# A bounded look-ahead for three engines between the gate stage and the second merge, and another order of the output's loads and last rows

## The chip, the cores and the metric

One core of a Trainium2 chip runs the whole kernel in one launch. The engines of the core have a queue of instructions each: TensorE (PE: matmuls, with its weight loads shown as PEld), VectorE (DVE), ScalarE (ACT), GpSimd (POOL) and SyncE (SP, which here only issues DMAs). The metric is the device time of one execution in microseconds. Each engine executes its queue in the order in which the kernel's scheduler has put it there; what an instruction at the head of a queue waits for, everything behind it waits for too.

## The reference

One step of a hybrid flow-matching backbone with a single layer, for 128 context tokens ("prompt") and 2048 latent tokens ("sample"), model width 1024. One input projection feeds three mixers of width 512:

```python
xn = rmsnorm(x, ln_g) * (1 + scale) + shift
qkv, beta, dec, z_a, u_b, v_b, z_b, x_c, z_c, gates = split(xn @ w_in)
# A: gated DeltaNet in chunks, forwards and backwards over the tokens, 4 heads of 128
#    S_t = a_t (I - b_t k_t k_t^T) S_{t-1} + b_t k_t v_t^T,   o_t = S_t^T q_t
o_a = rmsnorm(o) * silu(z_a)
o_b = u_b * (w_spatial @ rmsnorm(v_b) + b_spatial) * silu(z_b)   # chunks of 128 tokens
o_c = fourier(x_c) * silu(z_c)                                   # real part of a 2D (+ channel) FFT
merged = sum_n sigmoid(gates_n) * (o_n @ w_branch_n)
y = rmsnorm(x + gate * (merged @ w_out), final_g)
```

Results are y for both groups and the last states of the context scan.

## The kernel before

All big products are done in pairs of float16 (a high and a low half, three matmuls for one): `xh`, `xl` hold the modulated tokens, `whi`, `wlo` one block of 128 columns of a weight, scaled by a power of two that is found from the block's sum of squares. A weight block thus goes through a DMA, a square on ACT, a sum by one small matmul (`wscb`, `ones`), a few VectorE steps and the two conversions before TensorE may use it.

The stages follow each other on TensorE:

1. Prelude and SiLU gate stage (`silu_za`, `finish`), up to line 786: ACT, VectorE and TensorE are *kept* in written order here, by the wrapper `_InTurn`.
2. Decays and convolutions, the spatial mixer (`silu_unit`, `gate_unit`), the Fourier mixer (its tiles are `xc`, `Y1`, `X2`, `us`, `yT`; `halves_of` splits into pairs), then `merge(1)` and `merge(2)`, which multiply branch blocks (`big`) with `bhi`, `blo`, apply sigmoid gates `sg` and add rows `mrow`.
3. Beside all this runs `delta()`, a generator whose parts `pace.tick` and `pace.part` strew between the matmuls of stage 2. It first makes the triangular matrices (`n`, `T`, `tok`, inverted by VectorE in steps over `XB` and `E`, and stored as `ES`), then scans: for each of 34 chunks `S,sk` (state times keys), `v,R` (solve), `u,kn` (new state) are dependent matmuls with VectorE and ACT steps between them (`sv`, `u`, `S`), and `u,sqk`, `S,sq` and `finish(t, o)` make the output: squares `oss` on ACT, a power on GpSimd, scaling `o` on ACT, transposes on TensorE.
4. `merge(0)` and the output stage: eight pairs of token tiles (`two_tiles`), each a product of `pa` (merged, in seven linear combinations) with `wohi`, `wolo` or sums `tw` of the weight's quarters, then gate, residual, norm and store. The prompt's rows come last (`prompt_right`).

Between line 787 and the end the order on each engine is decided by the framework's scheduler, which has a timeline model: an instruction is put into its queue when the model says that its operands are there, so that instructions written much later can get ahead of earlier ones. `tc.high_priority()` moves one up; `tc.issue_after(x)` keeps an instruction behind `x` in its queue. The wrapper uses that:

```python
        def call(*args, **kw):
            with self.tc.issue_after(self.last.ins) if self.last is not None else ExitStack():
                self.last = f(*args, **kw)
```

In the output stage the loads at its start are chained by `in_turn`, which orders each SP load behind the one before. In the issue order on SP a load also waits until the load eight places earlier has landed.

Of the kernel before, what the change touches and what calls it, by code (L numbers as in the profile page):

```python
# [14 lines left out]
AF = mybir.ActivationFunctionType  # L15
ALU = mybir.AluOpType
# [4 lines left out]
P = 128  # L21
# [167 lines left out]
def hybrid_flow_kernel(ctx: ExitStack, tc: tile.TileContext, x_prompt, x_sample, state_delta, c, c_ctx, w_ada,  # L189
                       b_ada, w_blk, w_bd, a_log, dt_bias, w_spatial, b_spatial, w_brb, w_outb, final_g, w_adb, cols, x_t, x_tp,  # L190
                       consts, consts16, y_prompt, y_sample, new_state, dbg=None):
    nc = tc.nc
    G, SY = nc.gpsimd, nc.sync
    V, A, PE = [_InTurn(tc, e_) for e_ in (nc.vector, nc.scalar, nc.tensor)]
    uid, rot = [0], [0]

    def nm(s):
# [1758 lines left out]
    def sums_of(q):  # L1956
        in_turn(tw[q].rearrange("p j l k c -> p j (l k c)"), tD[q])
# [35 lines left out]
    def two_tiles(t, pa, xr, hh, end):  # L1993


        pl = ps_d if odd_pair[0] else ps_mm
        odd_pair[0] ^= 1
        a, Y, X = [bank(pl, [P, 512]) for _ in range(3)]
        p1 = sb(ep, [P, 512], "sg", bufs=4)
        u2, u3 = [sb(ep, [P, 512], "st", bufs=3) for _ in range(2)]  # L2000

        def gated(j, cs):
            G.tensor_tensor(hh[j][:, cs], hh[j][:, cs], gb[:, cs], ALU.mult)
            G.tensor_tensor(hh[j][:, cs], hh[j][:, cs], xr[j][:, cs], ALU.add)
# [36 lines left out]
        with tc.high_priority():  # L2041
            gate_add(hh[1][:, left], Y, gb[:, left], p1)
            piece(1, 1, xr[1], hh[1], left, V)
        Z = bank(ps_mm, [P, 512])
        product(Z, pa, 6, quarter(4, 512), True)
        with tc.high_priority():
            made = gate_add(hh[0][:, right], Z, gb[:, right], u2)
            piece(0, 1, xr[0], hh[0], right, V)
        with tc.issue_after(made.ins):
            for j, i in ((1, 0), (0, 0), (1, 1), (0, 1)):  # L2050
                summed_up(j, i)
        for j in (1, 0):
            G.tensor_tensor(norms[:, j:j + 1], parts[j][:, 1:2], mhalf, ALU.pow)
            A.activation(hh[j], hh[j], AF.Copy, scale=norms[:, j:j + 1])
            SY.dma_start(y_sample[0, (t + j) * P:(t + j + 1) * P], hh[j])

    parts = [sb(op, [P, 3], f"part{j}", bufs=1) for j in range(3)]
    norms = sb(op, [P, 3], "norms", bufs=1)

    def piece(j, i, junk, h, cs, on):  # L2060
        squared = A.activation(junk[:, cs], h[:, cs], AF.Square, accum_out=parts[j][:, i:i + 1])
        if on is not None:
            on.tensor_tensor(h[:, cs], h[:, cs], fg[:, cs], ALU.mult)
        return squared

    def summed_up(j, i):
        q_ = parts[j]
# [2 lines left out]
        else:  # L2070
            V.tensor_scalar(q_[:, 0:1], q_[:, 0:1], 1.0 / D, EPS, ALU.mult, ALU.add)

    def gate_add(out, src, gate, other):
        V.tensor_tensor(out, src, gate, ALU.mult)
        return V.tensor_tensor(out, out, other, ALU.add)

    def prompt_left():
        ps = bank(ps_mm, [P, 512])
# [4 lines left out]
        A.activation(gp[0], x_left, AF.Square, accum_out=parts[2][:, 0:1])  # L2083

    def prompt_right():
        after = None
        for i, cs in ((1, slice(0, 384)), (2, slice(384, 512))):
            ps = bank(ps_mm, [P, cs.stop - cs.start])
            gemm_N(ps, *p16, wo, 512 + cs.start, cs.stop - cs.start)
            with tc.high_priority(), tc.issue_after(after.ins) if i > 1 else ExitStack():  # L2090
                after = gate_add(gp_right[:, cs], ps, gp_right[:, cs], x_right[:, cs])
                A.activation(x_right[:, cs], gp_right[:, cs], AF.Square, accum_out=parts[2][:, i:i + 1])
                (G if i == 1 else V).tensor_tensor(gp_right[:, cs], gp_right[:, cs], fg[:, 512 + cs.start:512 + cs.stop], ALU.mult)
# [7 lines left out]
        V.tensor_scalar(gp_right, gp_right, n_, None, ALU.mult)  # L2101
        SY.dma_start(y_prompt[0, :, right], gp_right)

    in_turn(x_left, xp_[0:P, left])
# [52 lines left out]
```

## Time and profile before

| | us |
|---|---|
| median of 3 runs | 2162.39 (2161.81 to 2163.25) |
| profiled execution | 2166.18 |
| its span in the trace | 2164.4 |
| PE busy | 2088.8 (97%) |
| DVE busy | 1357.1 (63%) |
| ACT busy | 1061.7 (49%) |
| POOL busy | 751.7 (35%) |

The profiled execution is 1.8 us longer than its span and 3.8 us longer than the median. TensorE is busy 97% of the span, so what can be saved at an unchanged number of matmuls lies in the 76 us in which it is idle and in the stretches in which the granted clock is below 1. By the page the mean granted clock is 0.991. In the trace's answers a wait is shown as "idle before <- releaser", where the releaser is the instruction or DMA that ended it.

### The profile page before, as it was taken

The numbers are of one execution on the slowest core, as the hardware profiler recorded it, in microseconds if no ns is written. First come the engines' busy times: TensorE is split into PE (matmuls) and PEld (weight loads), VectorE is DVE, ScalarE is ACT, GpSimd is POOL, SyncE is SP. The second block draws the span as 40 slices with busy tenths as digits, with TensorE's granted clock in tenths as the row PEclk, the third lists the DMA queues.
The fourth block names the chain that finished last, engine by engine and source line by source line (L and its number), as shares of the span: only waits on it lengthen the run. The fifth ranks groups of instructions, "written<-read, shape, count | busy, mean of one in ns | idle before, by whom it ended". The sixth has DMA issues, their size and how long they took to land.

```text
span 2164.4 us, 42587 instructions
## 1 busy us (share of the span) xinstructions
PE 2088.8 (97%) x16133; PEld 1197.1 (55%) x16133; DVE 1357.1 (63%) x3101; ACT 1061.7 (49%) x2457; POOL 751.7 (35%) x933
## 2 busy tenths in 40 slices
PE   7999999999999999999899999999999999999998
PEld 4455444455555677777455555566555444444444
DVE  6656754389878797466655546756555554666245
ACT  5554744476555664445544445656543343453112
POOL 0321332233333432443222233345443234334364
PEclk9999999999999999999899999999999999999999
DMA  9525732277776743444655555867664645456852
GB/s 350 218 77 195 258 114 89 82 230 218 247 228 218 236 147 93 125 146 120 224 175 168 162 172 166 269 211 213 191 189 135 204 167 177 166 196 241 329 204 103
DMA packets 222909, 403.24 MB, mean 186 GB/s; under 512 B 39720, under 2 KB 109632, under 8 KB 219888
## 3 DMA queue, kind: packets, MB, share of 16 engines
q1 hardware_dynamic: 167664, 290.84, 42.2%
q0 software_dynamic: 15216, 65.89, 8.0%
q10 hardware_dynamic: 39824, 43.79, 6.1%
q8 instruction: 127, 2.08, 0.4%
q14 instruction: 78, 0.64, 0.1%
HBM read 258.19 MB, written 142.24 MB: 185 GB/s over the span
## 4 chain that ended last, share of the span: by engine, by line
PE 47%; DMA 8%; DVE 5%; ACT 2%; issue 1%; POOL 1%; SPq 0%; POOLq 0%; DVEq 0%; ACTq 0%
PE b L244 47%; DMA st<-br 2%; DMA pa<-pa 1%; DMA ES<-ei 1%; DMA br<-o 1%; DMA xh<-in_x_sample_dram 1%; DMA ei<-XB 1%; DVE big L1684 1%; DMA mrg<-mrow 0%; DMA S<-in_state_delta_dram 0%; DMA skn<-kv 0%; ACT big L1683 0%; PE b L1373 0%; DMA sn<-n 0%; DVE sg L470 0%
## 5 line engine op out<-in xcount | busy, mean ns | idle before, releaser
L244 PE MATMUL b<-xh,whi 128*128 128x512 f16 (+1 forms) x1920 | 650.9, 348 | 4.7 <-DVE sg L1447 2.5
L244 PE MATMUL b<-xl,whi 128*128 128x512 f16 (+1 forms) x1920 | 651.2, 348 | 0.0
L244 PE MATMUL b<-xh,wlo 128*128 128x512 f16 (+1 forms) x1920 | 650.6, 348 | 0.0
L244 PEld LDWEIGHTS <-whi 128*128 128x128 f16 x3888 | 355.6, 98 | 328.4 <-issue 11.8
L244 PEld LDWEIGHTS <-wlo 128*128 128x128 f16 x1944 | 190.5, 98 | 175.4 <-issue 3.8
L244 PE MATMUL b<-big,bhi 128*128 128x512 f16 (+1 forms) x960 | 251.5, 348 | 3.9 <-ACT big L1683 3.2
L244 PE MATMUL b<-big,blo 128*128 128x512 f16 (+1 forms) x480 | 163.3, 347 | 0.0
L1727 POOL TENSOR_TENSOR mrow<-mrow,sg 128x512 f32<-128x512 f32 (+1 forms) x80 | 93.0, 1163 | 145.9 <-DVE sg L1726 105.2
L244 PEld LDWEIGHTS <-xh 128*128 128x128 f16 x1496 | 119.0, 99 | 31.7 <-issue 2.5
L244 PEld LDWEIGHTS <-bhi 128*128 128x128 f16 x960 | 86.9, 98 | 77.9 <-ACT big L1683 2.9
L947 POOL TENSOR_TENSOR cy<-cy,raw 128x545 f32<-128x545 f32 (+1 forms) x48 | 64.1, 1361 | 182.4 <-ACT raw L946 182.4
L244 PEld LDWEIGHTS <-xl 128*128 128x128 f16 x1068 | 99.0, 99 | 44.6 <-DMA tw<-tw 2.0
L1717 ACT ACTIVATE sg<-b,winv 128x512 f32<-128x512 f32 (+1 forms) x120 | 74.0, 617 | 95.4 <-PE b L244 94.8
L1181 POOL COPY T<-ES 32x256 f16<-32x256 f16 x68 | 30.6, 450 | 198.0 <-DMA ES<-ei 189.8
L244 PE MATMUL b<-whi,xh 128*128 128x128 f16 x544 | 95.4, 222 | 2.7 <-DVE yT L1633 2.0
L244 PE MATMUL b<-wlo,xh 128*128 128x128 f16 x544 | 95.4, 222 | 0.0
L244 PE MATMUL b<-whi,xl 128*128 128x128 f16 x544 | 95.4, 222 | 0.0
L322 DVE SCALAR_TENSOR_TENSOR wlo<-wst,wsc,whi 128x1024 f16<-128x1024 f32 x52 | 67.7, 1303 | 34.1 <-ACT whi L321 34.0
L321 ACT ACTIVATE whi<-wst,wsc 128x1024 f16<-128x1024 f32 x52 | 59.4, 1145 | 51.4 <-DVE wsc L272 49.5
L1726 DVE SCALAR_TENSOR_TENSOR sg<-b,binv,sg 128x512 f32<-128x512 f32 (+1 forms) x80 | 53.4, 669 | 36.4 <-PE b L244 33.2
L1288 POOL TENSOR_TENSOR skn<-skn,ed 128x512 f32<-128x512 f32 x34 | 38.0, 1116 | 109.6 <-DMA skn<-kv 104.5
L244 PEld LDWEIGHTS <-pa 128*128 128x128 f16 x420 | 41.4, 99 | 54.5 <-DMA pa<-pa 3.8
(526 smaller groups left out, 4313.6 us busy)
## 6 DMA issues: line engine op xcount, KB each, us to landing
wst<-in_w_blk_dram SPq DMA_DIRECT2D x58, 512.0 KB, 3.9
pa<-pa POOLq DMA_DIRECT2D x16, 896.0 KB, 4.6
qkv<-cy POOLq DMA_DIRECT2D x12, 1089.0 KB, 5.3
st<-br SPq DMA_DIRECT2D x48, 256.0 KB, 3.6
mrow<-mrg SPq DMA_DIRECT2D x16, 576.0 KB, 4.6
pa<-pa SPq DMA_DIRECT2D x5, 1792.0 KB, 8.6
dc<-dec SPq DMA_DIRECT2D x17, 512.0 KB, 4.7
kq<-qkv SPq DMA_DIRECT2D x34, 256.0 KB, 4.9
```

The costliest lines, as they stand in the source:

```text
L244: newest[0] = PE.matmul(out, l, r, start=start, stop=stop, skip_group_check=reopened)
L321: w.made = A.activation(w.hi, st, AF.Copy, scale=s)
L322: w.low = V.scalar_tensor_tensor(w.lo, st, s, w.hi, ALU.mult, ALU.subtract)
L947: G.tensor_tensor(y[:, c0:c1], y[:, c0:c1], raw[:, 1 + c0:1 + c1], ALU.mult)
L1181: G.tensor_copy(T16[rows(a0, b), :, :, b], ES[0:32, :, 2 * a0 + b, :, wT])
L1288: G.tensor_tensor(h3(kn_), h3(kn_), bc(ed[:, d, t, :], P), ALU.mult)
L1684: V.scalar_tensor_tensor(o16[:, 1, g, t0:t0 + tn], st, s, o16[:, 0, g, t0:t0 + tn], ALU.mult, ALU.subtract)
L1717: gated_[0] = A.activation(sg, ps, AF.Sigmoid, scale=gw.inv)
L1726: V.scalar_tensor_tensor(sg, ps, binv[:, 1:2], sg, ALU.mult, ALU.mult)
L1727: G.tensor_tensor(mr, mr, sg, ALU.add)
```

## The change

Four edits. **The windows.** `_InTurn` keeps a list of what it issued. With `kept` each instruction is ordered behind the last one as before; with a `window` of n it is ordered behind the n-th last. From the end of the gate stage to the end of `merge(2)` ACT and GpSimd have a window of 4 and VectorE of 6; GpSimd is wrapped for that. TensorE is left to the scheduler, as is the rest of the kernel. **The loads.** The second pair's `pa` load comes ahead of `fg`, and the loads of `gp_right` and `x_right` go behind the third pair. **The last pair.** ACT, VectorE and TensorE are kept in written order from the last pair's second half on; one gate product and sum goes to GpSimd, the multiplies by `fg` change engines and places, and each row's root stands right behind its sum. **The prompt's right half** is written in the same way: the three sums and the root come ahead of the last multiply.

```diff
 class _InTurn:
     def __init__(self, tc, engine):
-        self.tc, self.engine, self.kept, self.last = tc, engine, False, None
+        self.tc, self.engine, self.kept, self.window, self.newest = tc, engine, False, 0, []
+
+    @property
+    def last(self):
+        return self.newest[-1] if self.newest else None
     def __getattr__(self, name):
         f = getattr(self.engine, name)
-        if not self.kept:
+        back = 1 if self.kept else self.window
+        if not back:
             return f
         def call(*args, **kw):
-            with self.tc.issue_after(self.last.ins) if self.last is not None else ExitStack():
-                self.last = f(*args, **kw)
-            return self.last
+            with self.tc.issue_after(self.newest[-back].ins) if len(self.newest) >= back else ExitStack():
+                self.newest.append(f(*args, **kw))
+            return self.newest[-1]
...
-    G, SY = nc.gpsimd, nc.sync
-    V, A, PE = [_InTurn(tc, e_) for e_ in (nc.vector, nc.scalar, nc.tensor)]
+    SY = nc.sync
+    G, V, A, PE = [_InTurn(tc, e_) for e_ in (nc.gpsimd, nc.vector, nc.scalar, nc.tensor)]
...
     V.kept = A.kept = PE.kept = False
+    A.window = G.window = 4
+    V.window = 6
...
     inv_ = merge(2, False, inv_, finish_delta, then=(0, 17), step=norm_step)
     cs_.close()
+    A.window = G.window = V.window = 0
...
+        in_order(True)
         total(u2, X, u2)
-        gate_add(p1, p1, gb[:, left], xr[1][:, left])
-        gate_add(hh[1][:, right], hh[1][:, right], gb[:, right], xr[1][:, right])
-        piece(1, 0, xr[1], hh[1], right, G)
-        gate_add(u2, u2, gb[:, right], xr[0][:, right])
-        piece(0, 0, xr[0], hh[0], left, G)
+        add_gated(u2, u2, gb[:, right], xr[0][:, right], G)
+        add_gated(p1, p1, gb[:, left], xr[1][:, left], V)
+        add_gated(hh[1][:, right], hh[1][:, right], gb[:, right], xr[1][:, right], V)
+        squared(1, 0, xr[1], hh[1], right)
+        squared(0, 0, xr[0], hh[0], left)
         product(Y, pa, 2, summed(3), False)
-        with tc.high_priority():
-            gate_add(hh[1][:, left], Y, gb[:, left], p1)
-            piece(1, 1, xr[1], hh[1], left, V)
         Z = bank(ps_mm, [P, 512])
         product(Z, pa, 6, quarter(4, 512), True)
-        with tc.high_priority():
-            made = gate_add(hh[0][:, right], Z, gb[:, right], u2)
-            piece(0, 1, xr[0], hh[0], right, V)
-        with tc.issue_after(made.ins):
-            for j, i in ((1, 0), (0, 0), (1, 1), (0, 1)):
-                summed_up(j, i)
+        final(hh[0], hh[0], left, left, V)
+        final(hh[1], hh[1], right, right, G)
+        summed_up(1, 0)
+        summed_up(0, 0)
+        add_gated(hh[1][:, left], Y, gb[:, left], p1, V)
+        squared(1, 1, xr[1], hh[1], left)
+        final(hh[1], hh[1], left, left, G)
+        add_gated(hh[0][:, right], Z, gb[:, right], u2, V)
+        squared(0, 1, xr[0], hh[0], right)
+        summed_up(1, 1)
+        root(1, 1)
+        final(hh[0], hh[0], right, right, V)
+        summed_up(0, 1)
+        root(0, 1)
         for j in (1, 0):
-            G.tensor_tensor(norms[:, j:j + 1], parts[j][:, 1:2], mhalf, ALU.pow)
             A.activation(hh[j], hh[j], AF.Copy, scale=norms[:, j:j + 1])
             SY.dma_start(y_sample[0, (t + j) * P:(t + j + 1) * P], hh[j])
...
     def prompt_right():
-        after = None
-        for i, cs in ((1, slice(0, 384)), (2, slice(384, 512))):
+        cols = slice(0, 384), slice(384, 512)
+        summed_up(2, 0)
+        for i, cs in enumerate(cols):
             ps = bank(ps_mm, [P, cs.stop - cs.start])
             gemm_N(ps, *p16, wo, 512 + cs.start, cs.stop - cs.start)
-            with tc.high_priority(), tc.issue_after(after.ins) if i > 1 else ExitStack():
-                after = gate_add(gp_right[:, cs], ps, gp_right[:, cs], x_right[:, cs])
-                A.activation(x_right[:, cs], gp_right[:, cs], AF.Square, accum_out=parts[2][:, i:i + 1])
-                (G if i == 1 else V).tensor_tensor(gp_right[:, cs], gp_right[:, cs], fg[:, 512 + cs.start:512 + cs.stop], ALU.mult)
-        with tc.issue_after(after.ins):
-            for i in range(3):
-                summed_up(2, i)
-        n_ = norms[:, 2:3]
-        G.tensor_tensor(n_, parts[2][:, 2:3], mhalf, ALU.pow)
-        A.activation(x_left, x_left, AF.Copy, scale=n_)
+            add_gated(gp_right[:, cs], ps, gp_right[:, cs], x_right[:, cs], V)
+            squared(2, 1 + i, x_right, gp_right, cs)
+        final(gp_right, gp_right, cols[0], slice(512, 896), V)
+        summed_up(2, 1)
+        summed_up(2, 2)
+        root(2, 2)
+        final(gp_right, gp_right, cols[1], slice(896, D), V)
+        A.activation(x_left, x_left, AF.Copy, scale=norms[:, 2:3])
...
     sums_of(3)
+    next_pair(in_turn)
     in_turn(fg, final_g[None, :].to_broadcast([P, D]))
-    in_turn(gp_right, gateD[1:2, right].to_broadcast([P, 512]))
-    in_turn(x_right, xp_[0:P, right])
-    next_pair(in_turn)
     prompt_left()
...
         if i == 0:
             next_pair(in_turn)
+            in_turn(gp_right, gateD[1:2, right].to_broadcast([P, 512]))
+            in_turn(x_right, xp_[0:P, right])
```

`squared`, `final`, `root` and `add_gated` are the former steps of `piece`, the power and `gate_add`, with the engine as an argument.

What the change moves is best seen in the queues. On VectorE, in the Fourier mixer's last quarter (`xc` is the low half of a projected tile, `XB` the copy that starts the inversion of the third group of triangular blocks), before:

```order
L1447 TENSOR_SCALAR sg_9561<-b_9536,zs_8303,sg_9561 128x128
L1100 COPY XB_9689<-XB_9689 64x1024
L1563 TENSOR_SCALAR xc_9671<-b_9574,xc_9671 128x512
L1107 TENSOR_TENSOR XB_9689<-XB_9689,E_9690 128x31
L1108 TENSOR_TENSOR E_9690<-E_9690,XB_9689 128x31
```

and after (through the wrapper every instruction has the wrapper's line):

```order
L188 TENSOR_SCALAR n_1221_9680<-n_1220_9678,n_1221_9680 128x512
L188 TENSOR_SCALAR xc_9671<-b_9574,xc_9671 128x512
L188 TENSOR_SCALAR xc_9790<-b_9693,xc_9790 128x512
L188 TENSOR_SCALAR wsc_9812<-b_9810 128x1
L188 TENSOR_SCALAR Y_1213_9571<-b_9793,Y_1213_9571 128x64x8
L188 TENSOR_SCALAR wsc_9812<-wsc_9812 128x1 x2
L188 TENSOR_TENSOR winv_9816<-wsc_9812,xsc_382 128x1
L188 TENSOR_SCALAR wlo_9675<-wst_8991,wsc_9812,whi_9674 128x1024
L188 TENSOR_SCALAR xc_9915<-b_9818,xc_9915 128x512
L188 COPY XB_9689<-XB_9689 64x1024
```

The copy of XB stood one place ahead of the low half of `xc_9671`, and now stands eight places behind it.

On TensorE, at one of the last steps of the scan, the last `v,R` matmuls (they make `b_21953`, from which VectorE and ACT make `u_21967`), before:

```order
L244 MATMUL b_21953<-v_2568_21813,R_1272_10504 128x128
L244 LDWEIGHTS Q_10514
L244 MATMUL b_22206<-R_1306_10912,Q_10514 128x64
L244 LDWEIGHTS Q_10514
L244 MATMUL b_22206<-R_1306_10912,Q_10514 128x64
L244 LDWEIGHTS sqk_21632
L244 MATMUL b_21926<-u_21650,sqk_21632 128x128
```

and, 75 rows on, the first `u,kn` matmul of the same step:

```order
L244 MATMUL b_22237<-xh_94,wlo_21568 128x512
L244 LDWEIGHTS whi_21567
L244 MATMUL b_22237<-xh_94,whi_21567 128x512
L244 LDWEIGHTS kn_2566_21793
L244 MATMUL b_22014<-u_21967,kn_2566_21793 128x128
```

After:

```order
L250 MATMUL b_21953<-v_2568_21813,R_1272_10504 128x128
L250 LDWEIGHTS R_1272_10504
L250 MATMUL b_21953<-v_2568_21813,R_1272_10504 128x128
L250 LDWEIGHTS kn_2566_21793
L250 MATMUL b_22014<-u_21967,kn_2566_21793 128x128
```

Between the two groups stood 22 matmuls of 512 columns and 20 small ones; now nothing stands there. The number of matmuls of the kernel is the same, 16,049; TensorE's order differs at some 17,500 of its rows.

On SP, at the start of the output stage, before:

```order
L1948 DMA tw_3065_25690<-tw 128x4096 x2
L1948 DMA fg_25689<-in_final_g_dram 128x1024
L1948 DMA xl_95<-gate 128x512
L1948 DMA xl_95<-in_x_prompt_dram 128x512
L1948 DMA pa_25706<-pa 128x4x1792
L1948 DMA xh_94<-in_x_sample_dram 128x1024 x2
L1954 DMA xl_95<-pa 128x4x1792
```

and after:

```order
L1957 DMA tw_3065_25690<-tw 128x4096 x2
L1957 DMA pa_25703<-pa 128x4x1792
L1957 DMA fg_25689<-in_final_g_dram 128x1024
L1957 DMA xh_94<-in_x_sample_dram 128x1024 x2
L1963 DMA xl_95<-pa 128x4x1792
L1976 DMA xh_94<-in_x_sample_dram 128x1024 x2
L1984 DMA out_dram<-xh_94 128x1024
L1957 DMA pa_25736<-pa 128x4x1792
L1957 DMA xl_95<-gate 128x512
L1957 DMA xl_95<-in_x_prompt_dram 128x512
```

`pa` of the second pair takes the place of `fg`, and the prompt's gate and rows stand behind the third pair's `pa`.

More of the change, by code (lines that the diff above doesn't have):

```diff
@@ L2052, in two_tiles, with in_order @@
+        summed_up(1, 1)
[3 more added lines that the diff above has]
+        root(0, 1)
         for j in (1, 0):
-            G.tensor_tensor(norms[:, j:j + 1], parts[j][:, 1:2], mhalf, ALU.pow)
             A.activation(hh[j], hh[j], AF.Copy, scale=norms[:, j:j + 1])
             SY.dma_start(y_sample[0, (t + j) * P:(t + j + 1) * P], hh[j])
+    def in_order(kept):
+        V.kept = A.kept = PE.kept = kept
     parts = [sb(op, [P, 3], f"part{j}", bufs=1) for j in range(3)]
@@ L2058, in hybrid_flow_kernel, with squared, final @@
     norms = sb(op, [P, 3], "norms", bufs=1)
[L2060 to L2064, printed above, removed]
+    def squared(j, i, junk, h, cs):
+        A.activation(junk[:, cs], h[:, cs], AF.Square, accum_out=parts[j][:, i:i + 1])
+    def final(out, h, cs, fs, on):
+        on.tensor_tensor(out[:, cs], h[:, cs], fg[:, fs], ALU.mult)
@@ L2071, in summed_up, with root, add_gated @@
             V.tensor_scalar(q_[:, 0:1], q_[:, 0:1], 1.0 / D, EPS, ALU.mult, ALU.add)
-    def gate_add(out, src, gate, other):
-        V.tensor_tensor(out, src, gate, ALU.mult)
-        return V.tensor_tensor(out, out, other, ALU.add)
+    def root(j, i):
+        G.tensor_tensor(norms[:, j:j + 1], parts[j][:, i:i + 1], mhalf, ALU.pow)
+    def add_gated(out, src, gate, other, on):
+        on.tensor_tensor(out, src, gate, ALU.mult)
+        on.tensor_tensor(out, out, other, ALU.add)
     def prompt_left():
@@ L2085, in prompt_right @@
     def prompt_right():
-        after = None
-        for i, cs in ((1, slice(0, 384)), (2, slice(384, 512))):
+        cols = slice(0, 384), slice(384, 512)
+        summed_up(2, 0)
+        for i, cs in enumerate(cols):
             ps = bank(ps_mm, [P, cs.stop - cs.start])
             gemm_N(ps, *p16, wo, 512 + cs.start, cs.stop - cs.start)
-            with tc.high_priority(), tc.issue_after(after.ins) if i > 1 else ExitStack():
-                after = gate_add(gp_right[:, cs], ps, gp_right[:, cs], x_right[:, cs])
-                A.activation(x_right[:, cs], gp_right[:, cs], AF.Square, accum_out=parts[2][:, i:i + 1])
-                (G if i == 1 else V).tensor_tensor(gp_right[:, cs], gp_right[:, cs], fg[:, 512 + cs.start:512 + cs.stop], ALU.mult)
-        with tc.issue_after(after.ins):
-            for i in range(3):
-                summed_up(2, i)
-        n_ = norms[:, 2:3]
-        G.tensor_tensor(n_, parts[2][:, 2:3], mhalf, ALU.pow)
-        A.activation(x_left, x_left, AF.Copy, scale=n_)
+            add_gated(gp_right[:, cs], ps, gp_right[:, cs], x_right[:, cs], V)
[6 more added lines that the diff above has]
+        A.activation(x_left, x_left, AF.Copy, scale=norms[:, 2:3])
         A.dma_start(y_prompt[0, :, left], x_left)
-        V.tensor_scalar(gp_right, gp_right, n_, None, ALU.mult)
+        V.tensor_scalar(gp_right, gp_right, norms[:, 2:3], None, ALU.mult)
         SY.dma_start(y_prompt[0, :, right], gp_right)
```

## The prediction

> **What bounds the kernel now.** I read the stages first, then TensorE's waits, then the queues behind the longest of them, then the end. Columns of the stages: window, its length, busy time and instructions of PE, PEld, DVE, ACT and POOL, granted clock, DMA share, GB/s.
>
> ```profile
> 550.00:1000.00 450.00, 427.36 (x4504) 302.09 (x4503) 336.16 (x847) 245.22 (x675) 168.00 (x229) 0.99 0.56 173
> 1110.00:1370.00 260.00, 259.83 (x2359) 154.83 (x2357) 150.59 (x397) 125.52 (x311) 72.22 (x113) 1.00 0.56 175
> 1370.00:1726.00 356.00, 340.79 (x2786) 196.56 (x2785) 207.56 (x518) 183.99 (x501) 144.04 (x169) 0.99 0.63 198
> 1726.00:2000.00 274.00, 274.00 (x1498) 132.60 (x1498) 162.26 (x363) 119.78 (x204) 107.12 (x118) 1.00 0.54 188
> 2000.00:2026.00 26.00, 21.63 (x92) 8.96 (x91) 7.33 (x11) 3.57 (x8) 12.12 (x11) 0.93 1.02 405
> 2150.40:2164.40 14.00, 5.04 (x47) 3.45 (x45) 7.24 (x19) 5.04 (x11) 4.27 (x5) 0.79 0.29 114
> ```
>
> TensorE is full from 1110 to 1370 and from 1726 to 2000, so other engines can be moved there for nothing as long as they stay in time. It has holes from 550 to 1000 (22.6 us), from 1370 to 1726 (15.2), in the first 26 us of the output stage (4.4), and after its last matmul. The waits of TensorE between 550 and 1730 (total, times, longest) say who makes them:
>
> ```profile
> PE b L1373 <- ACT o L1369: 4.4, 3, 2.7
> ...
> PE b L244 <- DVE sg L1447: 3.3, 4, 1.6
> ...
> PE b L244 <- DVE T L1045: 3.1, 4, 1.2
> PE b L244 <- DVE xc L1563: 2.7, 1, 2.7
> ...
> PE b L244 <- DVE yT L1633: 2.0, 1, 2.0
> ...
> PE b L244 <- ACT S L1224: 1.8, 1, 1.8
> ...
> PE b L1010 <- DVE n L1058: 1.7, 1, 1.7
> PE b L244 <- DVE u L1225: 1.4, 2, 1.0
> ...
> PE b L244 <- DVE X L1618: 1.1, 2, 0.6
> ```
>
> Each is a helper engine that is late though it is half idle. The two clearest cases on VectorE, from its timeline (start, length, what, idle time before):
>
> ```profile
> 829.27 1.06 DVE L1100 COPY XB<-XB 64x1024 f32<-64x1024 f32 x1 [6.08 <-DMA XB<-nd]
> 830.36 0.69 DVE L1563 SCALAR_TENSOR_TENSOR xc<-b,xc 128x512 f16<-128x512 f32 x1
> ...
> 880.25 0.49 DVE L1342 TENSOR_SCALAR S<-S,usc 128x512 f32<-128x512 f32 x1 [2.59 <-DMA S<-in_state_delta_dram]
> ```
>
> VectorE stood 6.08 us for a load of XB with the low half of xc queued behind it, and TensorE stood 2.7 us for xc. At 880 it stood 2.59 us for a state's load with yT behind it (2.0 on TensorE). The copy of XB is written after xc in the program; the scheduler let it overtake. That is what a bounded look-ahead can remove.
>
> Such a wait costs more than itself. After the two of them, and after the output stage's wait, the rows show half the clock:
>
> ```profile
> 830.87:834.28 3.41, 3.17 (x31) 3.17 (x32) 3.03 (x13) 1.48 (x4) 1.12 (x2) 0.50 0.28 96
> 882.07:885.48 3.41, 3.41 (x36) 3.41 (x34) 0.94 (x3) 1.46 (x3) 1.71 (x5) 0.50 0.60 184
> 2022.12:2025.53 3.41, 3.41 (x10) 1.17 (x9) 2.59 (x3) 0.58 (x2) 0.56 (x1) 0.50 1.03 419
> ```
>
> In 3.41 us at 0.50 half of the work is done, 1.7 us are lost.
>
> **The windows: what they give.** In the changed order XB's copy stands eight rows behind xc, and the state's scaling no longer ahead of yT. So xc gives 2.7 + 1.7, yT 2.0 + 1.7. GpSimd has a case of its own:
>
> ```profile
> 1540.66 0.83 POOL L1181 COPY T<-ES 32x256 f16<-32x256 f16 x2 [6.69 <-DMA ES<-ei]
> ...
> 1542.78 1.04 POOL L254 TENSOR_TENSOR oss<-oss,mhalf 128x4 f32<-128x4 f32 x1
> ```
>
> The root oss, on which ACT's o and then TensorE's 2.7 us wait hang, stood behind two copies that waited 6.69 us for ES. In the changed order copies from the same ES still stand in front of it (some written 7 and 11 instructions later: only the fourth last instruction is waited for, so four independent strings run ahead of each other). I leave these 2.7 us where they are, and take the other two waits on o, 4.4 − 2.7 = 1.7. The waits on X (1.1) and the longer one on u (1.0) were also overtakings. Of sg, T and n together (3.3 + 3.1 + 1.7 = 8.1) about half stand behind work that moves back: 4.0. Sum: 4.4 + 3.7 + 1.7 + 1.1 + 1.0 + 4.0 = 15.9 us; between 4 (xc alone) and 20.
>
> On the clock the Trainium skill speaks otherwise. "TensorE: Matmul & The Clock Gate", Part 1, section "HAM oscillation — how this bites in real kernels", has as its rule no idle gaps above about 3.4 us. By that the removed waits of 2.0 and 2.7 us would save only themselves, and the sum would be 3.4 us smaller. The rows at 830.87 and 882.07 disagree with it, 0.50 after waits of 2.7 and 2.0 us, so I keep the rows.
>
> **The windows: what they take.** Held back, ACT and VectorE can no longer start early, and TensorE's own order was planned anew around that. The delta chain goes from v,R matmuls to u, to u,kn matmuls, to S, to S,sk matmuls. Between the matmuls of two links stands other TensorE work, which must be longer than the link on the helpers:
>
> ```profile
> L1336 DVE SCALAR_TENSOR_TENSOR S<-S,egl,b 128x128 f32<-128x128 f32 x92 | 25.9, 342 | 11.5 <-PE b L244 11.2
> L1225 DVE SCALAR_TENSOR_TENSOR S<-S,S 128x512 f16<-128x512 f32 x24 | 20.1, 836 | 5.8 <-ACT S L1224 5.5
> ...
> L1225 DVE SCALAR_TENSOR_TENSOR u<-sv,u 128x512 f16<-128x512 f32 x26 | 18.4, 707 | 7.3 <-ACT u L1224 7.2
> L1319 DVE TENSOR_TENSOR sv<-b,beta 128x512 f32<-128x512 f32 x26 | 17.9, 688 | 10.8 <-PE b L244 10.7
> ```
>
> ```profile
> L1224 ACT ACTIVATE u<-sv 128x512 f16<-128x512 f32 x26 | 16.3, 628 | 21.1 <-DVE sv L1319 18.6 <-PE b L244 1.7 <-DVE binv L1693 0.6
> ...
> L1224 ACT ACTIVATE S<-S 128x512 f16<-128x512 f32 x24 | 15.1, 628 | 9.9 <-DVE S L1336 8.0 <-DVE S L1342 1.6
> ```
>
> The first link needs 0.69 + 0.63 + 0.71 = 2.0 us, the second three steps of 0.34 (the first of four goes beside matmuls) + 0.63 + 0.84 = 2.5. A matmul is priced by this row, taking 216 ns of 512 columns and a quarter of it for 128 (its twelve end 2.75 us after their start with the last one's tail):
>
> ```profile
> 2006.19 2.75 PE L244 MATMUL b<-xl 128*128 128x512 f16 x12
> ```
>
> Counted in the order, before has at least 2.5 us of TensorE work in all first links, and 1.7 and 1.2 in its two shortest second ones, where the trace has the 1.8 us wait on S. After has five short first links, 0.7, 1.3, 1.1, 1.7 and 0.0 us, short by 1.3 + 0.7 + 0.9 + 0.3 + 2.0 = 5.2; and seven short second ones, 0.8, 0.3, 0.6, 0.9, 2.2, 2.4, 2.4, short by 1.7 + 2.2 + 1.9 + 1.6 + 0.3 + 0.1 + 0.1 = 7.9. Less the 1.8 already paid, 11.3 us. The merge's first weight scale is left 0.7 us of work ahead of its use where it had 9.4: with a multiply chain of a few small steps about 2 us. Together 13.3. Lower bound: 0, if the helpers' real lead hides it (a helper that is ahead has the operands of the link at once, but these links hang on matmuls just done, which speaks against it). Upper bound: counting every short turn-round of TensorE and a helper, the triangular solver's too, 26 us less the 4 before, 22. I take the chain's 13.3, since these are serial by the data. Windows in all: −15.9 + 13.3 = −2.6.
>
> **The output's loads.** The wait of TensorE, the chain that led to it, and the issue of the load that the change puts behind pa:
>
> ```profile
> 2021.43 0.39 PE L244 MATMUL b<-wohi,pa 128*128 128x512 f16 x1 [3.33 <-DMA pa<-pa]
> ```
>
> ```profile
> 1989.08 12.88 DMA xh<-in_x_sample_dram
> ...
> 2001.98 19.40 DMA pa<-pa
> ```
>
> ```profile
> 1994.29 0.48 SPq L1948 DMA_DIRECT2D fg<-in_final_g_dram  x1
> ```
>
> pa could be issued only when a row load from eight places before had landed, and then took 19.40 us beside 405 GB/s of other loads. Now it takes the place of fg, some 7.7 us earlier, and fg, gp_right and x_right (0.5 + 0.25 + 0.25 MB) come after it: 1.05 MB at 405 GB/s is 2.6 us. TensorE's wait falls from 3.33 to about 0.7, and the half clock at 2022 goes (1.7): −4.3. Ends: −5.0 if pa is in time, 0 if the queues share and pa's neighbours only swap. fg is first read near 2022, and by then it has 20 us to land; gp_right and x_right are used four pairs later.
>
> **The end.** The last sum waits behind a multiply by fg that it doesn't need, and the prompt's squares wait on ACT for two row scalings:
>
> ```profile
> 2157.91 0.89 DVE L2093 TENSOR_TENSOR xl<-xl,fg 128x128 f32<-128x128 f32 x1
> 2158.72 0.15 DVE L2069 SCALAR_TENSOR_TENSOR part<-part 128x1 f32<-128x1 f32 x1
> ```
>
> ```profile
> 2154.89 2.19 ACT L2054 ACTIVATE xh<-xh,norms 128x1024 f32<-128x1024 f32 x2 [1.22 <-POOL norms L2053]
> 2156.98 0.51 ACT L2092 ACTIVATE xl<-xl 128x384 f32<-128x384 f32 x1
> ```
>
> The multiply goes behind the root, beside GpSimd's pow: 2158.72 − 2157.91 = 0.8. Earlier roots let the scalings (1.22 us of waiting before them) start earlier, of which the squares get 0.4 before their own operands bind. −1.2; ends 0 and −2, as GpSimd takes two passes more.
>
> **Sum.** −2.6 − 4.3 − 1.2 = −8.1 us. On the profiled execution (2166.18, span 2164.4) that is 2158.1; the median of the runs is 2162.39, 3.8 below it, so 2154.3.
>
> **Rivals.** (a) Slower: the re-planned order is short everywhere. The links and the solver's turn-rounds cost their full 22 us, and about half of the removals come (−8), with the loads and the end as above: 22 − 8 − 5.5 = +8.5, 2170.9. For it: stage 1110 to 1370 had 0.17 us of holes, so any short link there is new loss. Against: the chain's short links lie mostly outside. It decides from the point where new waits exceed removed ones by 5.5 us. 0.23.
> (b) The windows do not bound what they say, being strings of every fourth or sixth instruction: no gain and no loss between 550 and 1726, only 5.5 from the output, 2156.9. For it: the ES copies still ahead of oss. 0.13.
> (c) The loads share the bandwidth, pa lands as late as before: −2.6 − 1.2 = −3.8, 2158.6. For it: DMA share of 1.02. 0.10.
> (d) More: the 2.7 us on oss and its 1.7 of clock also go, and half of the links are hidden: −15.9 − 4.4 + 6.7 − 5.5 = −19.1, 2143.3. 0.14.
> The forecast itself has 0.40.
>
> **Numbers.** About 0.2%, 4.3 us, is what a measurement of this kernel can tell from no change. Faster by more than that: most of the forecast (0.36), all of (d), most of (b) (0.10) : 0.60. Within it: the rest of the forecast and of (b), (c) but for a little, 0.16. Slower: (a) and tails of the others, 0.24. With most of the chance on one side, the range goes from just beyond (d), 2141, to (a), 2171; what is left out is a (d) with all turn-rounds hidden and an (a) with new half-clock stretches.
>
> **What would show it.** Right: no wait on xc near 829 or yT near 881; VectorE's 6.08 us before XB's copy gone or with nothing behind it that TensorE needs; new waits of 1 to 2 us on u and S of the delta chain, the largest at the last link before 1580; pa's wait under 1 us and a clock of 1.00 near 2022; last sum right behind the last square. Wrong: new holes on T, R and Q copies in 1110 to 1370, or a wait on tw near 2010 above 1.03 us before the loads' gain appears, or the waits on oss gone altogether.

## The result: 9% slower, and the profile after

The changed kernel takes 2358.6 us (median of four runs), 196 us more than the kernel before in the same session (2162.8); the ratio is 1.091 (95% interval 1.089 to 1.093). The profiled execution took 2368.17 us, the longest of the four, with a span of 2366.4, 202.0 more than before. The page's head, busy times and waits of TensorE:

```profile
span 2366.4 us, 42558 instructions
PE 2153.4 (91%) x16133; PEld 1219.1 (52%) x16133; DVE 1365.7 (58%) x3100; ACT 1058.9 (45%) x2457; POOL 748.5 (32%) x934
```

The profile counts the same 16133 instructions of TensorE. It is busy 64.6 us longer (2153.4 against 2088.8) and idle for 213.0 us where it was for 75.6: 64.6 + 137.4 = 202.0. The other engines do about the same work (VectorE is busy for 8.6 us more, ACT and GpSimd for 3 less). TensorE's longer busy time goes with the clock, 0.961 on average instead of 0.991. The stages of the two kernels (bounds by the same landmarks: convolutions up to the last reading `raw`, then up to the first merge, `merge(1)` and `merge(2)`, `merge(0)`), first before, then after; columns as in the prediction:

```profile
153.10:415.40 262.30, 262.30 (x1451) 128.51 (x1448) 149.68 (x177) 137.26 (x196) 70.16 (x87) 1.00 0.42 148
415.40:1043.50 628.10, 599.39 (x5875) 407.06 (x5872) 482.29 (x1256) 350.45 (x982) 232.01 (x317) 0.99 0.59 180
1043.50:1731.10 687.60, 670.36 (x5660) 388.89 (x5661) 403.56 (x1023) 345.80 (x884) 232.25 (x306) 0.99 0.61 190
1731.10:1992.80 261.70, 261.70 (x1441) 127.01 (x1440) 153.65 (x342) 115.43 (x198) 101.59 (x112) 1.00 0.53 182
```

```profile
152.10:448.60 296.50, 268.84 (x1449) 129.85 (x1447) 142.10 (x174) 134.60 (x193) 68.58 (x88) 0.95 0.37 133
448.60:1145.20 696.60, 616.38 (x5796) 408.42 (x5794) 489.81 (x1239) 346.76 (x969) 228.28 (x313) 0.96 0.53 160
1145.20:1932.70 787.50, 712.48 (x5740) 408.26 (x5741) 411.10 (x1050) 350.95 (x901) 232.67 (x313) 0.94 0.54 168
1932.70:2196.10 263.40, 262.38 (x1442) 127.13 (x1441) 154.24 (x342) 115.94 (x198) 101.39 (x111) 1.00 0.52 180
```

+34 us in the convolutions, which were without a hole before; +69 up to the merges; +100 in the two merges under the windows; +2 where the windows are off. The waits of TensorE over the whole kernel are now many, on everything that ACT and VectorE make:

```profile
PE b L250 <- ACT raw L188: 27.7, 5, 11.1
PE b L250 <- DVE sg L188: 21.8, 15, 3.6
PE b L1381 <- ACT o L188: 11.3, 5, 3.6
PE b L250 <- ACT sg L188: 10.5, 13, 3.4
PE b L250 <- ACT S L188: 10.1, 5, 4.6
PE b L250 <- DVE vrow L188: 8.5, 2, 6.2
PE b L250 <- DVE mrow L188: 8.1, 7, 1.6
PE b L250 <- ACT u L188: 6.5, 5, 2.1
...
PE b L250 <- DVE u L188: 2.8, 6, 0.5
...
PE b L250 <- DVE xc L188: 2.0, 2, 1.8
...
PE b L250 <- DVE S L188: 1.7, 3, 0.7
```

The longest one shows the mechanism. `raw<-b` reads a finished sum out of its bank, which TensorE needs again. ACT's timeline, then TensorE's, then VectorE's:

```profile
197.03 1.28 ACT L188 ACT_TABLE_LOAD   x1 [0.39 <-ACT dc L188]
208.01 1.21 ACT L188 ACTIVATE raw<-cy 128x545 f32<-128x545 f32 x2 [9.70 <-DVE cy L188]
209.12 0.67 ACT L188 ACTIVATE raw<-b,winv 128x512 f32<-128x512 f32 x1
```

```profile
209.84 0.58 PE L250 MATMUL b<-xh,whi 128*128 128x512 f16 x1 [11.13 <-ACT raw L188]
```

```profile
199.68 1.23 DVE L188 TENSOR_TENSOR dc<-dc,tok 128x1024 f32<-128x1024 f32 x1 [4.13 <-DMA dc<-gamR]
200.82 2.48 DVE L188 SCALAR_TENSOR_TENSOR cy<-raw,pc,cy 128x2178 f32<-128x2178 f32 x1
```

The reading of 0.67 us is written behind the sigmoids of the tile before it (`raw<-cy`). These wait 9.70 us for VectorE's convolution `cy`, which itself stands behind a decay step that waits 4.13 us for a load. Before, the scheduler let such readings go ahead: the last reading of that tile (the first line here) had run before the same sigmoids came, and TensorE waited for none of them. ACT, before:

```profile
196.73 0.35 ACT L938 ACTIVATE raw<-b,winv 128x128 f32<-128x128 f32 x1
197.10 1.28 ACT L946 ACT_TABLE_LOAD   x1
198.58 2.30 ACT L946 ACTIVATE raw<-cy 128x545 f32<-128x545 f32 x4 [0.20 <-DVE cy L943]
```

A window of four does not allow that, and TensorE waits 11.13 us for 0.67 us of work. I looked up for each of TensorE's waits above 0.25 us what stood, without a pause, ahead of the instruction that ended it on its engine. Behind something written *earlier* were 19.4 us of waits before and 103.7 after; behind something written *later*, the case that the windows can mend, 9.5 before and 3.9 after; on the instruction's own operands 12.5 and 53.4. This takes each wait whole, not the part of it by which the instruction was held; and an operand can be late because its maker was held on another engine, so the last pair isn't a cause apart.

### The profile page after: what moved, and what is told of

Same layout as the page of the kernel before. It is cut to its first block, busy times and chain, and to the rows that moved or that the text cites. A ratio compares the mean times of both kernels' runs of the same rounds, so it can differ in the third digit from the quotient of the medians.

```text
span 2366.4 us, 42558 instructions
## 1 busy us (share of the span) xinstructions
PE 2153.4 (91%) x16133; PEld 1219.1 (52%) x16133; DVE 1365.7 (58%) x3100; ACT 1058.9 (45%) x2457; POOL 748.5 (32%) x934
## 5 line engine op out<-in xcount | busy, mean ns | idle before, releaser
L250 PE MATMUL b<-xh,whi 128*128 128x512 f16 (+1 forms) x1920 | 663.8, 354 | 59.4 <-ACT raw L188 27.7
L250 PE MATMUL b<-xl,whi 128*128 128x512 f16 (+1 forms) x1920 | 662.9, 354 | 0.0
L250 PE MATMUL b<-xh,wlo 128*128 128x512 f16 (+1 forms) x1920 | 660.3, 353 | 0.0
L250 PE MATMUL b<-big,bhi 128*128 128x512 f16 (+1 forms) x960 | 263.4, 363 | 18.8 <-ACT sg L188 10.5
L250 PEld LDWEIGHTS <-xh 128*128 128x128 f16 x1496 | 117.5, 98 | 37.5 <-issue 10.1
L188 ACT ACTIVATE sg<-b,winv 128x512 f32<-128x512 f32 (+1 forms) x140 | 85.6, 617 | 84.8 <-PE b L250 51.0
L188 POOL TENSOR_TENSOR mrow<-mrow,sg 128x512 f32<-128x512 f32 (+1 forms) x40 | 44.9, 1124 | 153.2 <-DVE sg L188 129.8
L188 ACT ACTIVATE raw<-cy 128x545 f32<-128x545 f32 (+2 forms) x56 | 44.9, 843 | 88.1 <-DVE cy L188 71.8
L188 ACT COPY nd<-n 32x128 f32<-32x128 f32 x136 | 40.0, 294 | 86.9 <-DVE n L188 75.2
L188 POOL DMA_DIRECT2D nd<-nd x34 | 26.8, 787 | 162.9 <-ACT nd L188 159.4
L250 PEld LDWEIGHTS <-blo 128*128 128x128 f16 x480 | 49.0, 102 | 47.4 <-issue 8.0
```

Of the source, the lines that this page charges most:

```text
L188: self.newest.append(f(*args, **kw))
L250: newest[0] = PE.matmul(out, l, r, start=start, stop=stop, skip_group_check=reopened)
```

## The experiments

Two theories on the windows. **E**: they hold late-written but urgent instructions behind earlier-written work that waits. **L**: they made the scheduler re-plan TensorE's own order, with too little between dependent matmuls (the step that the prediction priced). E was widened on the way, from readings of finished sums to everything urgent, and the expectations say so.

### The parts apart

All but the windows:

```diff
-    A.window = G.window = 4
-    V.window = 6
+    A.window = G.window = V.window = 0
```

> All of the change but the windows (they are 0 everywhere). Theory E (the windows keep helper engines from doing a late-written but urgent step first, evictions of finished sums above all) and theory L (the windows made the scheduler re-plan TensorE's own order, with too little work between dependent matmuls) both put the whole loss of 196 us into the windows: 2160 to 2164 us here, as the trace of the changed kernel has the first pair 3.0 us earlier in the output stage and 3.5 us more between the last matmul and the end. The prediction had 2157 (loads -4.3, end -1.2). Theory O (the output stage makes the loss): over 2200.

2161.97 us, ratio 0.9999 (0.998 to 1.001): no difference. The loss belongs to the windows. Inside the trace, the two parts of the output stage cancel: from the first product of the second pair to the last matmul 132.3 us instead of 134.0, that product 3.1 us sooner after the last merge (25.5 us instead of 28.6), and 12.4 us instead of 8.9 from the last matmul to the end.

One window each on the kernel before, `A.window = 4`:

> The kernel before with one window, ACT's of 4. Theory E: the trace of the changed kernel has some 85 us of TensorE's waits on ACT results and as much on VectorE's, 6 on GpSimd's, and half-clock stretches behind them; so +60 to +110 us, most of it in the convolution stage (raw) and the merges (sg, S, u): 2220 to 2270. Theory L: the loss lies in TensorE's order, which each window disturbs: about +65 from each engine, ACT no more than GpSimd.

2309.65 us, ratio 1.068 (1.065 to 1.071), +146.5. And `V.window = 6`:

> The kernel before with one window, VectorE's of 6. Theory E: +50 to +100 us, from sg, vrow, mrow, n and o behind earlier-written work; nothing in the convolution stage, whose evictions are ACT's: 2210 to 2260. Theory L: about +65, as for the others.

2307.58, ratio 1.067 (1.065 to 1.069), +144.4. And `G.window = 4`:

> The kernel before with one window, GpSimd's of 4. Theory E: GpSimd evicts nothing and nearly no wait of TensorE ends on it: within 15 us of before, perhaps a little faster as copies that wait for loads overtake less: 2150 to 2177. Theory L: about +65, 2228.

2160.98, ratio 0.9985 (0.9973 to 0.9998), −2.2. Both expectations for ACT and VectorE were too low, E's as well as L's 65: either window alone brings three quarters of the loss, and their sum (290) is far above the 196 of all three. A likely reason, not tried apart: most paths go through both engines in turn, and where one is held the other is late as well. VectorE's window costs 19 us even in the convolutions (281.6 us instead of 262.3), whose readings are ACT's, where E had said nothing: the sum of a weight block's squares is held there.

```profile
PE b L250 <- DVE wscb L188: 10.2, 3, 7.1
PE b L250 <- ACT whi L327: 4.3, 2, 3.8
PE b L250 <- DVE wlo L188: 2.6, 1, 2.6
```

GpSimd's window is the one that did not cost, as E had it and L did not. And it did change TensorE's order: in the queues of that kernel some 5,100 of the 16,049 matmuls stand in other places than before (9,900 with all three windows). Another order of TensorE is not a loss by itself.

### How wide

All three windows on the kernel before, with other widths than the change has:

```diff
-    A.window, V.window, G.window = 4, 6, 4
+    A.window, V.window, G.window = 16, 24, 16
```

> Windows four times as wide: 16 for ACT and GpSimd, 24 for VectorE. Theory E: what matters is how many instructions a reading must pass; in the convolution stage it is one set of sigmoids and decays, fewer than 16, so that stage comes back to 265; in the Fourier and merge stages VectorE's readings must pass the inversion's steps (31 pairs), so a third to a half of the loss stays: 2220 to 2270. Theory L: no more than a quarter of the loss goes, over 2300.

2193.66 us (two runs), ratio 1.014 (1.010 to 1.018), +30: less than either theory had, and not where E had it. The convolutions, which were to come back to 265, took 282.1 us; the stage up to the merges, which was to keep its loss, took 627.3 (628.1 before), the merges 697.7 (687.6). What is left in the convolutions are waits on the conversion of weight blocks, 13.1 of 13.8 us. With 64, 96 and 64:

> Windows of 64, 96 and 64. Theory E: almost everything that must pass can pass: within 20 us of before, 2160 to 2183. Theory L: still tens of us slower, as the wrapper's order itself disturbs the plan: over 2200.

2165.87, ratio 1.001 (0.999 to 1.003). The loss goes with the width: 196 (with the output's edits, which change nothing in the sum), 30, 2 us. The wrapper by itself costs nothing that these runs can tell; that instructions may pass some tens of others is what the kernel lives on.

### Who must pass

First only the convolutions' readings are set free: they are issued past the wrapper, under `urgent()`, a high priority that the window does not see.

```diff
-                with tc.high_priority():
+                with urgent():
                     A.activation(raw[:, o:o + tn], ps, AF.Copy, scale=w.inv)
```

> All three windows; of ACT only the 60 readings of the convolution stage (raw) stand outside. Theory E: that stage falls from 296 to 262-267 us and nothing else changes, 2358 - 32 = 2325 us. Theory L: the stage stays near 296.

2343.15 us (two runs), ratio 1.083 (1.079 to 1.088). The convolutions fell to 283.0, not to 262: half a hit. TensorE's waits in that stage say why:

```profile
PE b L260 <- ACT whi L190: 7.7, 2, 4.6
PE b L260 <- DVE wscb L190: 4.4, 2, 2.7
PE b L260 <- DVE wlo L190: 1.5, 2, 1.2
```

No wait on `raw` is left of 27.7 us, and 13.6 us on the conversion of the next weight block take their place, which is held in the same queues. So with all marked readings free:

> The kernel before with all three windows (4, 6, 4), but the instructions that the program marks as high priority (raw, sg, vrow, xc, mrow: readings of finished sums) stand outside of the windows, on ACT and VectorE. Theory E (late-written urgent readings are held behind earlier-written work): most of the loss goes, 2165 to 2230 us, and the convolution stage falls from 296 back to about 262 us. Theory C (the steps of the delta chain, which are not marked: n, o, S, u, R, T, are held as well, and the readings are only the ones that show): only the convolution stage comes back and some 30 to 50 us elsewhere, 2270 to 2300. Theory L (TensorE's order is re-planned badly whatever is held): over 2320.

2313.94 us, ratio 1.071 (1.066 to 1.075): in none of the three ranges, 84 us above E's, 14 above C's and 6 below L's. The convolutions, which E and C saw back, stayed at 283.9 us, and the merges hardly moved (778.5 after 787.5); what came back came in the stage between (662.5 after 696.6). This run doesn't decide between the theories. Then the weight conversions as well (`A.free` and `V.free` are the bare engines outside of the kept stages):

```diff
-        w.made = A.activation(w.hi, st, AF.Copy, scale=s)
-        w.low = V.scalar_tensor_tensor(w.lo, st, s, w.hi, ALU.mult, ALU.subtract)
+        w.made = A.free.activation(w.hi, st, AF.Copy, scale=s)
+        w.low = V.free.scalar_tensor_tensor(w.lo, st, s, w.hi, ALU.mult, ALU.subtract)
```

> As the kernel with the marked readings outside of the windows (2314 us), and the conversion of weight blocks outside as well (sum, scale, high and low half: wscb, wsc, whi, wlo, bhi, blo). Theory E, widened by what the run with raw alone free showed (raw's 27.7 us of waits became 13.6 on whi, wscb and wlo): the convolution stage comes back to 262-266 us, and with the weights of the later stages (wscb 11.5, whi 9.1 and wlo, bhi in that kernel's waits, with half-clock stretches behind them) 2314 - 45 = 2270 us, 2250 to 2290. Theory L: within 10 of 2314, with new waits in the old ones' place.

2259.3 us, ratio 1.045 (1.041 to 1.048): the sum is as E expected, the place is not. The merges gave 46 of the 55 us, and the convolutions stayed at 276.5 (TensorE waits 12.8 us for one reading, which the scheduler queued behind sigmoids and decay steps that are still held). And the scan's steps, from `level` to `finish`, in the same way:

> The steps of the delta scan outside of the windows too (sv, u, S, v, Q, R's and T's halves, o, of). Held are the inversion and preparation of the triangular matrices, the Fourier mixer's yT and X, the branch blocks (big) and all DMA issues on ACT, and GpSimd. Theory E: what is left to hold acts between 420 and 1050 us for the most part: 2190 to 2225 us, the merge stages back within 10 us of before (343, 345). Theory L: over 2250, and the merge stages stay 20 us or more above before, as TensorE's order comes from all windows.

2207.51 us, ratio 1.020 (1.017 to 1.023). Its stages:

```profile
154.00:429.80 275.80, 264.29 (x1450) 129.05 (x1448) 148.57 (x172) 139.81 (x196) 68.64 (x88) 0.98 0.40 141
429.80:1096.00 666.20, 610.91 (x5884) 411.07 (x5882) 491.73 (x1261) 349.94 (x986) 225.67 (x318) 0.96 0.56 170
1096.00:1773.90 677.90, 666.14 (x5653) 386.99 (x5652) 409.81 (x1024) 342.66 (x880) 237.96 (x308) 1.00 0.62 192
```

The two merges take 677.9 us and are no longer slower than before (687.6); what remains, +14 and +38, lies where held work remains (decays, the matrices' preparation, the Fourier mixer). So the loss goes where the hold goes, as E has it, in pieces: marked readings about 45 us, weights 55, the scan's steps 52, the rest 43. It does not rule L out inside the scan, for with the scan's steps free TensorE's own order came back too. Counted in the queues with the prediction's prices, TensorE's work in the links of the scan is 2.4 us short before, 16 in the changed kernel (the prediction's own count was 13.1), 26, 9 and 2.1 in the last three. Such sums are small beside 196 us, and from the first to the second of the three they fall by 17 us while the merges gain 46; but a kernel with TensorE's changed order and free helpers, which would part the two, was not run.

| kernel | us | above before | convolutions | up to the merges | two merges |
|---|---|---|---|---|---|
| before | 2162.8 | | 262.3 | 628.1 | 687.6 |
| all three windows and the output (the change) | 2358.6 | +196 | 296.5 | 696.6 | 787.5 |
| windows, marked readings free | 2313.9 | +150 | 283.9 | 662.5 | 778.5 |
| also weights free | 2259.3 | +94 | 276.5 | 661.6 | 732.8 |
| also the scan free | 2207.5 | +43 | 275.8 | 666.2 | 677.9 |

### The output stage

The loads alone, on the kernel before:

```diff
+    next_pair(in_turn)
     in_turn(fg, final_g[None, :].to_broadcast([P, D]))
-    in_turn(gp_right, gateD[1:2, right].to_broadcast([P, 512]))
-    in_turn(x_right, xp_[0:P, right])
-    next_pair(in_turn)
```

> The kernel before with the changed order of the output's loads alone. The profile of the changed output stage has the second pair's product 3.0 us earlier: -3 us with pa's wait under 1 us and no half clock near 2022 (2160.5); the prediction had -4.3. If the gain were only the bandwidth shared out in another way (rival c): within 1 us, with a longer wait on tw.

2157.73 us, ratio 0.9968 (0.9953 to 0.9983): faster by 0.3%, some 7 us (3.7 to 10), which is more than the 3 expected. In its trace the second pair has no wait on `pa`, and the wait on `tw` is 1.52 us (1.03 before):

```profile
2007.04 5.35 PE L244 MATMUL b<-tw,xl 128*128 128x512 f16 x24 [1.52 <-DMA tw<-tw]
```

From the end of the merges to the product of the second pair it takes 25.7 us instead of 28.6, and 132.3 from there to the last matmul instead of 134.0: 2.9 + 1.7 = 4.6 us. The rest of the 7 us can't be told from the spread of the runs.

With GpSimd's window as well:

> The two parts that did not lose, together: GpSimd's window of 4 and the new order of the output's loads, VectorE and ACT free, the end as before. If the two are independent: -2.2 - 3 = -5 us, 2158, faster by 0.25%.

2156.53, ratio 0.997 (0.995 to 0.999): nothing that can be told from the loads alone. These two kernels beat both the one before and the changed one; the loads are in both.

The end, +3.5 us where −1.2 was forecast. The time from the last matmul to the end of the span is steady enough to be read from one trace: 8.9 to 9.0 us in all twelve kernels with the end as before, 12.4 in both with the changed one. VectorE in the changed kernel, and what GpSimd did beside it:

```profile
2344.79 0.68 DVE L188 TENSOR_TENSOR sg<-sg,wst 128x512 f32<-128x512 f32 x1
2345.51 1.64 DVE L188 TENSOR_TENSOR sg<-sg,xh 128x512 f32<-128x512 f32 x1
2347.07 1.75 DVE L188 TENSOR_TENSOR xh<-xh,wst 128x512 f32<-128x512 f32 x1
...
2350.95 1.25 DVE L188 TENSOR_TENSOR xh<-xh,fg 128x512 f32<-128x512 f32 x1 [1.40 <-ACT xh L188]
...
2354.96 1.23 DVE L188 SCALAR_TENSOR_TENSOR part<-part 128x1 f32<-128x1 f32 x1
```

```profile
2344.96 1.64 POOL L2094 TENSOR_TENSOR st<-st,wst 128x512 f32<-128x512 f32 x1 [2.71 <-DVE st L188]
2346.68 1.59 POOL L2095 TENSOR_TENSOR st<-st,xh 128x512 f32<-128x512 f32 x1
```

Two things at once: passes that take 0.69 us alone take 1.64 and 1.75 beside GpSimd's, and the written order makes VectorE stand 1.40 us for ACT's square with the sums of the last products behind it. The first undone:

```diff
-        add_gated(u2, u2, gb[:, right], xr[0][:, right], G)
+        add_gated(u2, u2, gb[:, right], xr[0][:, right], V)
```

> Loads and end as changed, no windows, but the gate product and sum that the change gave to GpSimd (u2) back on VectorE. Measured by the time from the last matmul to the end of the span: 8.9 us before, 12.4 with the changed end. Theory P (VectorE and GpSimd slow each other: two sums on VectorE took 1.64 and 1.75 us beside GpSimd's where 0.69 is their length alone): VectorE has two passes more (1.4) and gains 2.0 and some of the wait behind: 11.4 to 12. Theory W (the loss is the written order on VectorE: the multiply of the first half row waits 1.40 us for ACT's square ahead of the sums that TensorE's last products need): 13 to 14.

11.8 us from the last matmul to the end instead of 12.4, as theory P has it and W has not: VectorE is done sooner with two passes more, as none of these six now takes over 0.69 us. The second undone (the gate sums of `Y` and `Z` and their squares ahead of all `final`, `summed_up(1, 0)` and `summed_up(0, 0)`):

> Loads and end as changed, no windows, but the gate sums of the last two products and their squares written ahead of the four multiplies by fg and of the first two sums of squares. Theory W: the wait of 1.40 us and the 1.25 us of the multiply leave VectorE's path to the last sums, the end falls by 2 to 2.7: 9.7 to 10.4 us after the last matmul. Theory P: the multiplies beside GpSimd's still cost as much, only later: within 0.7 of 12.4.

10.8 us, between the ranges of both. Each theory holds for a part, 0.6 and 1.6 us of the 3.5; the multiply that was moved then took 1.75 us beside GpSimd's. The rest was not tried apart.

## Why the prediction was wrong, point by point

**The windows' price** is the step that failed: "13.3", with "22" as its upper bound, where the runs have +196. The waits on u and S of the delta chain, which were to grow by 11.3 us, grew from 4.1 (1.8 on S by ACT, 1.4 and 0.6 on u, 0.3 on S by VectorE) to 21.1 (6.5 + 2.8 on u, 10.1 + 1.7 on S). That the size is near is in good part luck. In most links VectorE begins `sv` 0.04 us after the last `v,R` matmul; at the links that ended at 1518 and 1554 it began 2.47 and 3.06 us after it, held by other work, and TensorE then waited 1.9 and 2.6 us. Of the waits on u of over 1.5 us only the one after 1802 (2.2 us, `sv` 0.28 us late) is the short link that was priced. And the links were one wait of many. The upper bound was none: it set TensorE's work between two matmuls against the length of the helper's steps, as if the helper were free when the operands came. With a window the helper is not free: it stands for something else at the head of its queue. Readings, weight blocks and the scan each had to pass such heads.

**"Other engines can be moved there for nothing as long as they stay in time"** was said of stretches without a hole, and the convolutions were not priced at all; TensorE had no wait in them before, and they lost 34 us. That was the overtaking at work: a trace shows the overtakings that harm (9.5 us) and none of those that help.

**The gain of 15.9** did not come. The waits behind later-written work fell from 9.5 to 3.9 us, but the tiles that were to gain wait longer for other reasons: o for the root oss 11.3 us instead of 4.4, sg on VectorE 21.8 instead of 5.1. TensorE still waits 1.8 us for xc, now behind a copy of XB that is written earlier than it.

**The clock**: long waits are followed by half-clock stretches, as the prediction had it, and here that worked against the change: 185.9 us of the span are at 0.50 instead of 41.9, and 64.6 of 202 us are TensorE's longer busy time. That each wait of 2 to 3 us takes 1.7 us more is not so; the last section has the rule that the traces show.

**The output's loads**: right, −4.6 in the trace against −4.3, with pa's wait at 0 to 0.44 us instead of the forecast 0.7 and tw's 0.5 longer; rival (c) did not come. The 1.7 of clock in it is partly luck: with the old order of loads TensorE waited for pa 3.53 us in the kernel with the widest windows and 3.39 in the one with the weights free, and no half clock followed.

**The end**: wrong in sign, +3.5 for −1.2. It counted what left the last chain and took GpSimd's two passes as free; VectorE's passes beside them grew, and the wait of 1.40 us for a square was not looked for.

**Rival (a)** had the sign and the mechanism's place ("the re-planned order is short everywhere"), but with 8.5 us, as it used the same bound. Its reason, short links in TensorE's order, is too small for the loss: 16 us of missing work in the links against 196.

## What to carry to other kernels

Before an order is made stricter, look at what the present order lets pass: for every step that frees or feeds the bounding engine, count how many instructions it overtakes and what those wait for. A stage without a hole says nothing of how it would fare without that freedom. Bound a change to a queue by the waits of whatever can come to its head, not by the lengths of the steps.

## What the runs showed of the hardware

**VectorE beside GpSimd.** Passes of VectorE over 128x512 of which neither operand lay in a result bank of TensorE took 0.68 to 0.69 us when GpSimd ran nothing (eight of them in the traces before and after). Beside a pass of GpSimd some took no longer, others 0.95 to 1.75; a sum of one column took 1.23 us beside one (0.15 otherwise).

**The clock.** A wait of a given length does not decide whether the clock is halved; where it lies does. In the traces the granted clock changes only at borders 3.41 us apart, and whether a slot between two borders follows a slot at full clock at 0.50 goes by how long TensorE stood idle in that one. Two waits of the changed kernel, 1.95 us up to 223.88 and 1.94 us up to 1531.57, each lie across a border. The slots around them (the second number is TensorE's busy time, the third from the end the clock):

```profile
219.82:223.23 3.41, 2.11 (x10) 0.88 (x9) 0.00 (x0) 3.03 (x4) 1.18 (x3) 1.00 0.64 250
223.23:226.65 3.42, 2.77 (x13) 1.27 (x13) 0.00 (x0) 3.07 (x5) 0.00 (x0) 1.00 1.01 374
1527.13:1530.54 3.41, 1.80 (x16) 1.10 (x16) 2.43 (x5) 3.40 (x7) 0.00 (x0) 1.00 0.33 78
1530.54:1533.95 3.41, 1.44 (x12) 1.28 (x12) 2.46 (x6) 1.15 (x3) 1.97 (x2) 0.50 0.92 281
```

The first wait left 1.30 us of idle time in its first slot and 0.65 in its second, and the clock stayed at 1.00. The second came behind other waits, which made it 1.6 us in the slot up to 1530.54, and the half clock began there, while TensorE still stood. In the two traces, before and after, from 160 us to 30 us before the end, all 27 slots at full clock with 2.0 us or more of idle time were followed by a slot at 0.50, and none of the 1104 with up to 1.3; of the 28 between, 10 were. So the 2.7 us before 830.87 in the kernel before, 2.4 of them in one slot, cost the half clock, and 3.53 us for pa in the kernel with the widest windows, split into 1.6 and 1.9, did not. The 1.7 us that the prediction added to such a wait is what it can cost, not what each one costs.
